# Three edits to the order of work in a hybrid mLSTM, retention and feed-forward block: gate tables stored head by head, one product's operands in step order, own buffers at its first gate

## The chip, the cores and the metric

The kernel runs on one core of one Trainium2 chip. The metric is the device time of one execution in microseconds (us); for several runs of one kernel the median is given. A profile is one execution taken by the hardware profiler. PE is TensorE's matmul part, PEld its weight load, DVE VectorE, ACT ScalarE, POOL GpSimd, SP SyncE, which issues most DMAs from one queue.

## The reference, cut to what matters

One block of a streaming encoder in float32: 16 meta tokens and 1024 positions of width 1024. A token mixer of four mLSTM heads and four retention heads (128 wide keys, 256 wide values, computed in chunks) is followed by an output product, and then by a gated feed-forward part with a causal convolution.

```
proj = up @ w_in                       # q, k, v, o, i, f and the retention's q, k, v, g
li = GATE_CAP * jnp.tanh(i_pre / GATE_CAP);  lf = jax.nn.log_sigmoid(ml_f + ml_b_f)
h_ml = mlstm_chunkwise(q, k, v, li, lf)      # stabilised by a running maximum of the gates
h_rt = retention_chunkwise(rq, rk, rv, log_gamma)
mixed = concat([sigmoid(ml_o) * head_norm(h_ml), silu(rt_g) * head_norm(h_rt)])
h = h + (mixed @ w_out)                      # the output product
...
a = causal_dwconv(u @ w_up, ffn_conv_w)      # u = rmsnorm(h)
h = h + (jax.nn.silu(a) * (u @ w_gate)) @ w_down
return rmsnorm(h, norm_final_g)[:, N_META:]
```

## The kernel before

Every product is kept exact to float32 by splitting each operand into a high part (a cast on ACT) and a low part (a subtraction on DVE), and by three matmuls for each pair of tiles: high by high, high by low, low by high. They are the lines 924 to 926 (`mm3s`), and every row `hi_x`, `lo_x`, `wr`, `rr`, `uh_g`, `ul_g` is such a half of a weight or an activation. Lines 783 and 784 (`wsplit`) split weights; line 1339 (`rsplit`) splits the output product's activations.

Large products use seven block products instead of eight, with sums and differences of blocks as operands. The output product (`mixw`, an instance of `Seven` with the name "w") goes through the stages "1", "65", "73", "4" and "2", each of eight steps k. A step of "65" or "73" has two products: 12 matmuls of 128x512 into four banks "y" and 12 into four banks "x". `prep` makes the operands of a step: in stage "65" it splits A1 (to `wr_01` at step 0), replaces A1 by -A1-B2 and splits that (`wr_00`), and then by -A1-A2 in place for a later stage. The second of two steps that share a ring has its activations in the tiles `rr`. The weight blocks' sums lie in DRAM (`wsw`) and come to `wdraw`'s tiles: two "raw" tiles, and two tiles `wd` with two places each. B1, A1 and so on are loaded from DRAM as well (`wa`).

The mLSTM heads need, for each head, two tables A1 and A2 that repeat a row of 1040 gate values on all 128 partitions. `gates` computes them for all heads and chunks as 36 rows (chunk times 4 plus head) of 128 and stores them in one DRAM tile `scr`; `tables_load` reads a head's rows back, broadcast to all partitions. The `raw_vp` loads bring weights of the value projection; their cast `hi_vp` stands on ACT (line 475). Line 1598 masks a chunk's scores (`pt`).

After the output product the rows are scaled by their root mean square, in three column ranges; `xcomb` then makes the combined operands for the feed-forward part's seven-product form (blocks `xh`, `uh_g`, `ul_g`). The first pair of the up and gate weights is done plainly in eight products, before all combinations exist: `first_up` and `first_gate`, with names such as `pup_000` (weight half m, column half, range) and `pga_11` (weight half m, column half). A gate's weight half is split into the hi/lo ring, which has three places.

The order of work is decided when the program is built: `watch` adds up estimated loads and end times of every instruction, the planner deals out tasks by them, and a scheduler orders each engine's instructions by simulated times, within the dependences. `after` adds an order without a semaphore between two instructions of one engine (a NoSync dependence). On each queue, SP's too, instructions go in the order in which they stand.

Of the kernel before, what the change touches and what calls it, by code (L numbers as in the profile page):

```python
# [17 lines left out]
P = 128  # L18
# [6 lines left out]
H = 4  # L25
# [64 lines left out]
def body(ctx, tc, h_in, vecs, cst, mask_in, rot, w_v0, w_vp, w_g, w_out, w_up, w_gate, w_down, out):  # L90
# [17 lines left out]
    last = {}  # L108
    G, PE, V, AC = nc.gpsimd, nc.tensor, nc.vector, nc.scalar
    pinned = [False]  # L110
    load = {"PE": 0.0, "DVE": 0.0, "Activation": 0.0, "Pool": 0.0, "SP": 0.0, "wire": 0.0}
    before = {}
    TABLES = ("Sqrt", "Sigmoid", "Silu", "Exp")
# [18 lines left out]
    def watch(ins):  # L132
        eng, kind = ins.engine.name, type(ins).__name__
        if "Tile" in kind or not ins.outs or eng not in load:
            return
        dma = "DMA" in kind
        seen[0] += 1
        if not dma and eng in ("PE", "DVE", "Activation"):
            if pinned[0] and eng in before:
                tc.add_manual_dep(ins, before[eng], mybir.DependencyInfo(mybir.DependencyClass.NoSync, mybir.DependencyReason.DATA), reason="order")  # L140
            before[eng] = ins.name
        o = ins.outs[0]
        n = math.prod(x[1] for x in o.ap[1:])
        rd = [e for e in map(extent, ins.ins) if e]
        wr = [e for e in map(extent, ins.outs) if e]
        t = load[eng]
        why = None
        for e, w in [(e, False) for e in rd] + [(e, True) for e in wr]:
            for lo, hi, wrote, at, by in uses.get(e[0], ()):
                if lo < e[2] and hi > e[1] and (w or wrote):  # L150
                    x = at if by == eng and not dma else at + 0.05
                    if by == eng and not dma:
                        continue
                    if x > t:
                        t, why = x, (by, e[0])
        if eng == "PE" and t - load["PE"] > 0.25:
            stalls.append((t, t - load["PE"], wr[0][0], why))
        if dma:
            load[eng] = t + (0.4 if eng == "SP" else 0.1)
            size = n * o.ap[0][1] * 4e-6  # L160
            if eng == "SP":
                load["wire"] = max(load["wire"], t + 1.8) + size / 0.3 * (2 if "scr" in str(rd) else 1)
                end = load["wire"]
            else:
                load["wire"] += size / 0.3
                end = t + 1.8 + size / 0.15
        else:
            if eng == "PE":
                if F32 not in [x.dtype for x in ins.ins]:
                    c = max(0.107, 0.004 + 0.000445 * n)  # L170
                elif o.ap[0][1] == 32:
                    c = 0.13
                elif getattr(ins, "is_transpose", False):
                    c = 0.109
                else:
                    c = 2 * max(0.11, 0.00084 * n)
                whole = F32 in [x.dtype for x in ins.ins]
                c += 0.1 * (whole != kindof[0])
                kindof[0] = whole
                end = t + c + 0.165  # L180
            elif eng == "DVE":
                c = 0.07 + 0.00105 * n + (0.06 if "ScalarPtr" in kind else 0.0)
                end = t + c + 0.085
            elif eng == "Activation":
                c = 0.045 + 0.00093 * n + 0.1 * (len(ins.ins) - 1)
                f = ins.func.name if hasattr(ins, "func") else "Copy"
                if f in TABLES and f != table[0]:
                    table[0] = f
                    c += 1.3
                end = t + c + 0.1  # L190
            else:
                c = 0.15 + 0.0017 * n
                end = t + c
            load[eng] = t + c
            fin[0] = max(fin[0], end)
        for e, w in [(e, False) for e in rd] + [(e, True) for e in wr]:
            u = uses.setdefault(e[0], [])
            if w:
                u[:] = [x for x in u if x[0] < e[1] or x[1] > e[2]]
            else:  # L200
                u[:] = [x for x in u if x[2] or x[4] != eng or x[0] < e[1] or x[1] > e[2]]
            u.append((e[1], e[2], w, end, eng if not dma else "q" + eng))
# [39 lines left out]
    gts = st.tile([P, 2, NCH, H], F32, name="gts")  # L242
    ug = st.tile([P, KB, 32], F32, name="ug")
    mask = st.tile([P, P], F32, name="mask")
    scr = dram.tile([2, R36, P], F32, name="scr")

    def sig(b, p):
        t0, t1, _ = PIECES[p]
# [530 lines left out]
    def wsplit(hi, lo, srcs):  # L779
# [5 lines left out]
            o += n  # L785
        return hi, lo

    def fstep(u, s):
        kind, i = fseq[u]
        nm = f"{kind}{i}_{s}"  # L790
        fetch(u)
        (w11, w12, r0), (w21, w22, r1) = fraws[u]
        if s:
            fetch(u + 1)
        if u < 2:
            return fsplit(nm, [(r0, r1)[s]])
        if s == 0:
            return fsplit(nm, [r0])
        if s == 1:
            s1 = fpool[0].tile([P, HB], F32, tag="s1", name=f"s1_{u}", bufs=1)  # L800
            V.tensor_tensor(s1, w21, w22, ALU.add)
            V.tensor_tensor(w21, w21, w11, ALU.subtract)
            V.tensor_tensor(w11, s1, w11, ALU.subtract)
            return fsplit(nm, [w11, s1])
        if s == 2:
            V.tensor_tensor(w12, w12, w11, ALU.subtract)
            return fsplit(nm, [w21, w12])
        return fsplit(nm, [w22])
# [338 lines left out]
    def tables_load(h):  # L1147
        if h <= H + 1:
            tabs[0], tabs[1] = (st.tile([P, 2 * SB], F32, tag=f"A{i + 1}", name=f"A{i + 1}_{h}") for i in range(2))
        A1, A2 = tabs[0][:, :T], tabs[1][:, :T]  # L1150
        if h > H + 1:
            return
        if h >= H:
            nc.sync.dma_start(A1, rot[:, 0])
            nc.sync.dma_start(A2, rot[:, 1])
            tabs["at"] = load["wire"]
            return
        src = scr.rearrange("x (c h) t -> x h c t", h=H)
        for x, a in ((0, A1), (1, A2)):
            if x == 0:  # L1160
                nc.sync.dma_start(a[:, :META], src[x, h, 0, :META].partition_broadcast(P))
            nc.sync.dma_start(a[:, META:].rearrange("p (c t) -> p c t", t=P), src[x, h, 1:].partition_broadcast(P))
        tabs["at"] = load["wire"]

    def tables_tasks(h):
# [76 lines left out]
    def gates():  # L1242
# [72 lines left out]
        V.tensor_scalar(mc[:, 1:2], mc[:, 1:2], math.log(KSCALE), None, ALU.add)  # L1315
        e, wi, ws = w, li, lf
        V.tensor_scalar(e, cm, mc[:, 0:1], -1.0, ALU.max, ALU.mult)
        nc.sync.dma_start(scr[0], e)
        AC.activation(wi, e, AF.Exp, bias=mc[:, 0:1])
        nc.sync.dma_start(scr[1], wi)  # L1320
        AC.activation(ws, t, AF.Exp, bias=mc[:, 1:2])
        V.tensor_tensor(b, e, b, ALU.subtract)
        AC.activation(b, b, AF.Exp, scale=2.0)
# [30 lines left out]
    class Seven:  # L1354
# [52 lines left out]
            return V.tensor_tensor(self.act[a, k], self.act[b, k], self.act[c, k], ALU.subtract)  # L1407

        def prep(self, t):

            if t >= len(self.steps) or t in self.ops:
                return
# [14 lines left out]
            elif st in self.QUARTER:  # L1427
                if k % 2 == 0:
                    self.w = fsplit(nm, [d["w"]])
                r = self.right.get((st, k)) or rsplit(act[{"1": "A1", "2": "A2", "4": "A1"}[st], k], self.rt(st, k, 0))  # L1430
                self.ops[t] = [(half_of(self.w, k % 2), r, "xy"[st == "2"])]
            elif st == "65":
                a1, a2, b2 = (act[q, k] for q in ("A1", "A2", "B2"))
                r5 = rsplit(a1, self.rt(st, k, 1))
                V.scalar_tensor_tensor(a1, a1, -1.0, b2, ALU.mult, ALU.subtract)
                w = fsplit(nm, [d["l"]])
                r6 = rsplit(a1, self.rt(st, k, 0))
                V.scalar_tensor_tensor(a1, a1, -1.0, a2, ALU.mult, ALU.subtract)
                self.ops[t] = [(half_of(w, 0), r6, "x"), (half_of(w, 1), r5, "y")]
            else:  # L1440
                w = fsplit(nm, [d["l"]])
                r7 = rsplit(act["B1", k], self.rt(st, k, 0))
                r3 = rsplit(act["B2", k], self.rt(st, k, 1))
                self.ops[t] = [(half_of(w, 1), r7, "x"), (half_of(w, 0), r3, "y")]
# [67 lines left out]
    wcount = {"draw": 0}  # L1512

    def wdraw(st, nm):
        if st == "1" or nm in ("w65_0", "w65_1", "w65_2", "w65_3"):
            left = next((q for q in jfreed if q), None)
            return raw_tile(nm, left.pop(0) if left and st == "1" else None)
        if not wdraws:
# [501 lines left out]
    def xcomb(k, j0, j1):  # L2020
# [3 lines left out]
        u4, t3, t2 = (xtile(f"x{x}{k}_{j0}", n) for x in "utv")  # L2024
        AC.activation(u4, B4, AF.Copy, scale=g4)
        x = V.scalar_tensor_tensor(t3, B1, g1, u4, ALU.mult, ALU.subtract)
        if k or j0:
            after(x, last["scaled"])
        V.scalar_tensor_tensor(t2, A1_, g1, t3, ALU.mult, ALU.subtract)
        xput(4, k, j0, j1, t2)  # L2030
# [219 lines left out]
    def eight(kind, half, j0, j1, bank, done):  # L2250
        for m in range(2):
            hi, lo = need((kind, 0, m), 2 - m)
            pt = bank(m)[:, :j1 - j0]
            xs = [xb(kb // 4 if half == 0 else (6, 2)[kb // 4]) for kb in range(KB)]
            mm3s(pt, [tuple(y[:, kb * P:(kb + 1) * P] for y in (hi, lo)) for kb in range(KB)],
                 [tuple(y[:, kb % 4, j0:j1] for y in xs[kb]) for kb in range(KB)], True, True)
            done(m, pt)

# [339 lines left out]
```

## Time and profile before

| | |
|---|---|
| median of 3 runs | 1526.14 us (1525.41 to 1527.58) |
| profiled execution, first to last instruction (span) | 1523.9 us |
| what the median has beyond that span | 2.2 us |
| mean granted TensorE clock | 0.995 |
| busy: PE, DVE, ACT, POOL | 98%, 72%, 50%, 5% |
| matmuls | 9929 |
| HBM read and written | 178.05 and 67.15 MB |

A row of the timeline reads: start in us, duration in us, engine, line of the kernel, operation, output<-inputs, shape, how many; in brackets the idle time of the engine just before, and what ended it. Matmuls overlap: the distance of two starts is what one costs, its duration is longer. In the view of stretches a row has the bounds, the length, busy time and count for PE, PEld, DVE, ACT and POOL, and at the end the granted clock, the share of the 16 DMA engines and GB/s. A row of the transfers gives size and median time from issue to landing.

### The profile page before, as it was taken

The page shows a single profiled execution, that of the slowest core. Times are in us where ns is not written, and L with a number is a line of the kernel's source. Part 1 is how long each engine was busy: PE and PEld are TensorE (multiplying, and loading weights), DVE is VectorE, ACT ScalarE, POOL GpSimd, SP SyncE. Part 2 cuts the span into 40 slices and gives each one's busy share as a digit, 9 for nine tenths or more (in the row PEclk, how much of TensorE's full clock was granted, in tenths as well). Part 3 has the DMA queues.
Part 4 walks back from the last instruction along what each step waited for, and adds up shares of the span by engine and source line. Part 5 has one row for each costly group of instructions (what it writes and reads, how often), then busy time and mean ns, then how long its engine had stood idle before and what let it go on. Part 6 is the DMA issues. An engine that isn't in the chain of part 4 may idle for free.

```text
span 1523.9 us, 25488 instructions
## 1 busy us (share of the span) xinstructions
PE 1487.8 (98%) x9929; PEld 1349.9 (89%) x9929; DVE 1090.4 (72%) x2087; ACT 756.4 (50%) x1455; POOL 72.1 (5%) x157
## 2 busy tenths in 40 slices
PE   7989999999999999999999999999999999999997
PEld 7988999998999999987888998999999999888887
DVE  6885868677777677756867787766666666778667
ACT  4465655554655455544454565444444444344443
POOL 1000000000000000000000001222220000000000
PEclk9999999999999999999999999999999999999999
DMA  6022245323632446697333247887772224933213
GB/s 232 2 93 56 90 155 192 111 84 111 200 106 98 131 161 199 194 401 258 108 115 125 77 136 222 209 211 201 177 186 77 83 82 157 369 106 108 97 42 111
DMA packets 104586, 223.81 MB, mean 147 GB/s; under 512 B 10520, under 2 KB 33760, under 8 KB 104288
## 3 DMA queue, kind: packets, MB, share of 16 engines
q1 hardware_dynamic: 89824, 191.68, 37.4%
q0 software_dynamic: 8448, 23.07, 7.6%
q10 hardware_dynamic: 6192, 7.41, 1.4%
q8 instruction: 78, 1.28, 0.3%
q14 instruction: 44, 0.36, 0.1%
HBM read 178.05 MB, written 67.15 MB: 161 GB/s over the span
## 4 chain that ended last, share of the span: by engine, by line
PE 89%; DVE 5%; ACT 2%; DMA 2%; issue 1%; SPq 0%; DVEq 0%; ACTq 0%
PE pdx L926 3%; PE pdx L925 3%; PE pdx L924 3%; PE pup_x L925 2%; PE pup_x L924 2%; PE pup_x L926 2%; PE pga_x L924 2%; PE pga_x L925 2%; PE pga_x L926 2%; PE pdy L926 2%; PE pdy L925 2%; PE pdy L924 2%; PE n L1621 2%; PE pwx L926 2%; PE u L1619 2%; PE pwx L924 2%
## 5 line engine op out<-in xcount | busy, mean ns | idle before, releaser
L783 ACT CAST hi_up<-raw_up 128x512 fp32r<-128x512 f32 (+1 forms) x52 | 36.4, 719 | 106.7 <-PE pga_z L925 60.2
L924 PE MATMUL pup_x<-uh_g,hi_up 128*128 128x256 f32 (+1 forms) x240 | 67.6, 284 | 1.2 <-ACT uh_g L1995 1.2
L784 DVE TENSOR_TENSOR lo_up<-raw_up,hi_up 128x512 fp32r<-128x512 f32 (+1 forms) x52 | 41.3, 809 | 38.3 <-ACT hi_up L783 37.5
L784 DVE TENSOR_TENSOR lo_ga<-fraw_ga,hi_ga 128x512 fp32r<-128x512 f32 (+1 forms) x52 | 41.9, 808 | 37.3 <-ACT hi_ga L783 37.1
L925 PE MATMUL pup_x<-ul_g,hi_up 128*128 128x256 f32 (+1 forms) x240 | 67.7, 284 | 0.1
L926 PE MATMUL pup_x<-uh_g,lo_up 128*128 128x256 f32 (+1 forms) x240 | 66.5, 283 | 0.0
L784 DVE TENSOR_TENSOR lo_d<-rd,hi_d 128x1024 fp32r<-128x1024 f32 (+1 forms) x34 | 37.7, 1113 | 32.8 <-ACT hi_d L783 32.7
L783 ACT CAST hi_ga<-fraw_ga 128x512 fp32r<-128x512 f32 (+1 forms) x52 | 36.4, 719 | 45.5 <-PE pup_z L925 24.1
L926 PE MATMUL pdx<-uh_d,lo_d 128*128 128x512 f32 (+1 forms) x156 | 57.9, 375 | 0.0
L925 PE MATMUL pdx<-ul_d,hi_d 128*128 128x512 f32 (+1 forms) x156 | 57.8, 374 | 0.0
L783 ACT CAST hi_d<-rd 128x1024 fp32r<-128x1024 f32 (+1 forms) x34 | 32.3, 959 | 49.3 <-PE pdy L925 32.5
L926 PE MATMUL pdy<-uh_d,lo_d 128*128 128x512 f32 x132 | 51.9, 393 | 0.0
L925 PE MATMUL pdy<-ul_d,hi_d 128*128 128x512 f32 x132 | 51.7, 392 | 0.0
L924 PE MATMUL pdx<-uh_d,hi_d 128*128 128x512 f32 (+1 forms) x156 | 48.5, 372 | 0.0
L924 PE MATMUL pdy<-uh_d,hi_d 128*128 128x512 f32 x132 | 47.9, 389 | 0.0
L924 PEld LDWEIGHTS pup_x<-uh_g,hi_up 128*128 128x128 f32 x240 | 45.7, 191 | 2.3 <-ACT uh_g L1995 1.4
L924 PE MATMUL pga_x<-uh_g,hi_ga 128*128 128x512 f32 x120 | 47.5, 396 | 0.0
L925 PE MATMUL pga_x<-ul_g,hi_ga 128*128 128x512 f32 x120 | 47.5, 396 | 0.0
L926 PE MATMUL pga_x<-uh_g,lo_ga 128*128 128x512 f32 x120 | 47.1, 393 | 0.0
L925 PEld LDWEIGHTS pup_x<-ul_g,hi_up 128*128 128x128 f32 x240 | 45.8, 191 | 1.0 <-DVE ul_g L1996 0.3
L926 PEld LDWEIGHTS pup_x<-uh_g,lo_up 128*128 128x128 f32 x240 | 45.0, 190 | 0.7
L1688 DVE SCALAR_TENSOR_TENSOR mx<-tr,vec,sig 128x386 f32<-128x386 f32 (+2 forms) x42 | 24.0, 571 | 21.1 <-PE tr L1680 16.0
(1687 smaller groups left out, 5732.4 us busy)
## 6 DMA issues: line engine op xcount, KB each, us to landing
raw_up<-w_up_d SPq DMA_DIRECT2D x22, 512.0 KB, 5.6
fraw_ga<-w_gate_d SPq DMA_DIRECT2D x22, 512.0 KB, 4.3
acts<-cv SPq DMA_DIRECT2D x44, 256.0 KB, 4.6
wsd<-w_down_d POOLq DMA_DIRECT2D x44, 256.0 KB, 6.7
rd<-wsd SPq DMA_DIRECT2D x22, 512.0 KB, 3.5
raw_w<-w_out_d SPq DMA_DIRECT2D x20, 512.0 KB, 7.3
wsw<-raw_w SPq DMA_DIRECT2D x32, 256.0 KB, 3.1
raw_m<-w_out_d SPq DMA_DIRECT2D x14, 512.0 KB, 4.0
```

The lines of the kernel that those rows point to most:

```text
L783: AC.copy(hi[:, o:o + n], x)
L784: V.tensor_tensor(lo[:, o:o + n], x, hi[:, o:o + n].bitcast(F32), ALU.subtract)
L924: m.append(PE.matmul(pt, ah, xh_, start=first and k == 0, stop=False, skip_group_check=True))
L925: PE.matmul(pt, ah, xl_, start=False, stop=False, skip_group_check=True)
L926: m.append(PE.matmul(pt, al, xh_, start=False, stop=last and k == n - 1, skip_group_check=True))
L1619: PE.matmul(up[:, :nv], kw[:L], v, start=True, stop=True)
L1621: PE.matmul(pn[:L, :nv], pt[:L, :L], v, start=True, stop=c == 0)
L1688: return V.scalar_tensor_tensor(dst, tr[:, x0 - t0:x1 - t0], vec[:, g:g + 1], sig(b, p)[:, x0 - a0:x1 - a0], ALU.mult, ALU.mult)
```

## The change

A. `scr` becomes eight DRAM tiles of 9 rows, one for each table and head. `gates` writes them with eight stores instead of two, after both row sets are there. A head's table is then one contiguous piece of 4 KB for each partition instead of eight pieces of 512 B.

B. `prep` of the stages "65" and "73" of the output product puts its PE, DVE and ACT instructions into a chain, one for each engine, in the order in which they are issued (`row`, `rows65`). In stage "65" the weight split stands ahead of the first activation split. `wdraw` gives the two raw tiles to the weights of the steps 4 to 7 of stage "65"; before, steps 0 to 3 had them.

C. At the first gate the second weight half is split into four tiles of the ring "cv" instead of the hi/lo ring (`wsplit2`); `eight` takes it as two pieces. In `xcomb` the order behind the last scaled row holds for the second column range alone, no longer for k > 0 of the first.

```diff
+            if row and eng in row[0]:
+                tc.add_manual_dep(ins, row[0][eng], mybir.DependencyInfo(mybir.DependencyClass.NoSync, mybir.DependencyReason.DATA), reason="order")
+            if row:
+                row[0][eng] = ins.name
...
-    scr = dram.tile([2, R36, P], F32, name="scr")
+    scr = [[dram.tile([NCH, P], F32, name=f"scr{x}{h}") for h in range(H)] for x in range(2)]
...
+    def wsplit2(nm, x):
+        r = [[ctile(f"{p}{nm}_{i}", F32R) for i in range(2)] for p in ("hi", "lo")]
+        for i in range(2):
+            wsplit(r[0][i], r[1][i], [x[:, i * HB:(i + 1) * HB]])
+        return r
...
+        if (u, s) == (1, 1):
+            return wsplit2(nm, r1)
...
-            nc.sync.dma_start(a[:, META:].rearrange("p (c t) -> p c t", t=P), src[x, h, 1:].partition_broadcast(P))
+            nc.sync.dma_start(a[:, META:], scr[x][h][1:].rearrange("c t -> (c t)").partition_broadcast(P))
...
-        nc.sync.dma_start(scr[0], e)
         AC.activation(wi, e, AF.Exp, bias=mc[:, 0:1])
-        nc.sync.dma_start(scr[1], wi)
+        for h in range(H):
+            for x, y in enumerate((e, wi)):
+                nc.sync.dma_start(scr[x][h], y[h:R36:H])
...
         def prep(self, t):
+            if self.nm == "w" and t < len(self.steps) and self.steps[t][0] in ("65", "73"):
+                row.append(rows65)
+                self.make(t)
+                row.clear()
+            else:
+                self.make(t)
...
                 a1, a2, b2 = (act[q, k] for q in ("A1", "A2", "B2"))
+                w = fsplit(nm, [d["l"]])
                 r5 = rsplit(a1, self.rt(st, k, 1))
                 V.scalar_tensor_tensor(a1, a1, -1.0, b2, ALU.mult, ALU.subtract)
-                w = fsplit(nm, [d["l"]])
                 r6 = rsplit(a1, self.rt(st, k, 0))
...
-        if st == "1" or nm in ("w65_0", "w65_1", "w65_2", "w65_3"):
+        if st == "1" or nm in ("w65_4", "w65_5", "w65_6", "w65_7"):
...
-        if k or j0:
+        if j0:
             after(x, last["scaled"])
```

PE's row order is the same as before up to stage "65". Three places show what moves. On SP's queue where the gate tables are stored (`scr`; in the new names scr_119 to scr_122 hold the first table of heads 0 to 3, scr_123 to scr_126 the second), before:

```order
L329 DMA raw_vp_22_1270<-w_vp_d 128x1024
L329 DMA raw_q0b<-w_g_d 128x512 x2
L1318 DMA scr<-gates 36x128
L1320 DMA scr<-gates 36x128
L1161 DMA A_0_1704<-scr 128x16
L1162 DMA A_0_1704<-scr 128x8x128
L1162 DMA A_0_1705<-scr 128x8x128
L329 DMA raw_vp_11_1266<-w_vp_d 128x1024
L329 DMA raw_vp_12_1304<-w_vp_d 128x1024
```

And on SP's queue at the same place now:

```order
L1333 DMA scr_125<-gates 9x128
L1333 DMA scr_122<-gates 9x128
L1333 DMA scr_126<-gates 9x128
L334 DMA raw_vp_11_1279<-w_vp_d 128x1024
L334 DMA raw_vp_12_1317<-w_vp_d 128x1024
L1173 DMA A_0_1717<-scr_119 128x16
L1174 DMA A_0_1717<-scr_119 128x1024
L1174 DMA A_0_1718<-scr_123 128x1024
L334 DMA raw_o0a<-w_g_d 128x1024
```

Head 0's two tables have moved behind the two raw_vp loads, which follow the eight stores directly.

On ACT at the start of stage "65" (hi_w_0 and so on are the weights of step 0 and on, wr_01 and wr_00 the activations of step 0, rr those of step 1, wr_21 those of step 2), before:

```order
L783 CAST hi_w_6_8323<-raw_w_6_8063 128x1024
L783 CAST hi_w_0_8418<-raw_w_0_8069 128x1024
L1339 CAST rr_8358<-wa_8375 128x512
L783 CAST hi_w_1_8448<-raw_w_1_8188 128x1024
L1339 CAST rr_8357<-wa_8375 128x512
L783 CAST hi_w_2_8488<-raw_w_2_8265 128x1024
L1339 CAST wr_01_8414<-wa_8375 128x512
L1339 CAST wr_00_8422<-wa_8375 128x512
```

And on ACT now:

```order
L788 CAST hi_w_6_8335<-raw_w_6_8076 128x1024
L788 CAST hi_w_0_8425<-wd_8082 128x1024
L1352 CAST wr_01_8429<-wa_8386 128x512
L1352 CAST wr_00_8433<-wa_8386 128x512
L788 CAST hi_w_1_8455<-wd_8082 128x1024
L1352 CAST rr_8369<-wa_8386 128x512
L1352 CAST rr_8368<-wa_8386 128x512
L788 CAST hi_w_2_8495<-wd_8083 128x1024
```

Step 0's activations have moved ahead of the weights of steps 1 and 2. On DVE, whose rows follow the same order, wr_01's low part now stands behind the last residual additions of stage "1" and the last mixing rows (`wa`, `mm`):

```order
L789 TENSOR_TENSOR lo_w_0_8426<-wd_8082,hi_w_0_8425 128x1024
L1709 SCALAR_TENSOR_TENSOR wa_8279<-tr_1_1_8331,vec,sig 128x126
L1709 SCALAR_TENSOR_TENSOR wa_8326<-tr_1_1_8331,vec,sig 128x258
L1496 TENSOR_TENSOR resid_8136<-resid_8136,pwx_8140 128x512
L1496 TENSOR_TENSOR resid_8136<-resid_8136,pwx_8144 128x512
L1496 TENSOR_TENSOR resid_8137<-resid_8137,pwx_8159 128x512
L1709 SCALAR_TENSOR_TENSOR wa_8326<-tr_2_0_8348,vec,sig 128x254
L1709 SCALAR_TENSOR_TENSOR mm<-tr_2_0_8348,vec,sig 128x2
L1496 TENSOR_TENSOR resid_8137<-resid_8137,pwx_8175 128x512
L1709 SCALAR_TENSOR_TENSOR wa_8326<-tr_2_1_8356,vec,sig 128x254
L1709 SCALAR_TENSOR_TENSOR mm<-tr_2_1_8356,vec,sig 128x2
L1352 TENSOR_TENSOR wr_01_8429<-wa_8386,wr_01_8429 128x512
```

Before, lo_w_1 and lo_w_2 and the first step-1 activation stood among these rows, ahead of wr_01's low part.

On PE at the first gate, before, the end of the gate's first product (pga_01) and what follows:

```order
L926 MATMUL pga_01_9855<-xh_9052,lo_ga_0_9732 128x512
L924 MATMUL pup_000_9911<-uh_g,hi_up_0_9418 128x256
L924 MATMUL pup_100_9938<-uh_g,hi_up_1_9426 128x256
L925 MATMUL pup_000_9911<-ul_g,hi_up_0_9418 128x256
L926 MATMUL pup_000_9911<-uh_g,lo_up_0_9419 128x256
```

And on PE now:

```order
L939 MATMUL pga_01_9872<-xh_9065,lo_ga_0_9745 128x512
L937 MATMUL pga_11_9900<-xh_9067,higa_1_0_9860 128x512
L938 MATMUL pga_11_9900<-xl_9068,higa_1_0_9860 128x512
L939 MATMUL pga_11_9900<-xh_9067,loga_1_0_9862 128x512
L840 MATMUL pcb_9646<-cs,Rb 128x1 x2
L937 MATMUL pga_11_9900<-xh_9067,higa_1_0_9860 128x512
```

The 24 matmuls of pga_11 have moved from behind the second column range of the up product to the front; pup_000, pup_100, pga_00 and pga_10 follow them, and the second range (pup_001 and on) comes after those.

More of the change, by code (lines that the diff above doesn't have):

```diff
@@ L110, in body @@
     pinned = [False]
+    row, rows65 = [], {}
     load = {"PE": 0.0, "DVE": 0.0, "Activation": 0.0, "Pool": 0.0, "SP": 0.0, "wire": 0.0}
@@ L1157, in tables_load @@
             return
-        src = scr.rearrange("x (c h) t -> x h c t", h=H)
         for x, a in ((0, A1), (1, A2)):
             if x == 0:
-                nc.sync.dma_start(a[:, :META], src[x, h, 0, :META].partition_broadcast(P))
-            nc.sync.dma_start(a[:, META:].rearrange("p (c t) -> p c t", t=P), src[x, h, 1:].partition_broadcast(P))
+                nc.sync.dma_start(a[:, :META], scr[x][h][0, :META].partition_broadcast(P))
+            nc.sync.dma_start(a[:, META:], scr[x][h][1:].rearrange("c t -> (c t)").partition_broadcast(P))
         tabs["at"] = load["wire"]
@@ L1409, in prep, with make @@
         def prep(self, t):
+            if self.nm == "w" and t < len(self.steps) and self.steps[t][0] in ("65", "73"):
[4 more added lines that the diff above has]
+                self.make(t)
+        def make(self, t):
             if t >= len(self.steps) or t in self.ops:
@@ L2254, in eight @@
             xs = [xb(kb // 4 if half == 0 else (6, 2)[kb // 4]) for kb in range(KB)]
-            mm3s(pt, [tuple(y[:, kb * P:(kb + 1) * P] for y in (hi, lo)) for kb in range(KB)],
+            mm3s(pt, [tuple(y[kb // 4][:, kb % 4 * P:(kb % 4 + 1) * P] if type(y) is list else y[:, kb * P:(kb + 1) * P] for y in (hi, lo)) for kb in range(KB)],
                  [tuple(y[:, kb % 4, j0:j1] for y in xs[kb]) for kb in range(KB)], True, True)
```

## The prediction

> **What bounds the kernel now.** I read the page first: busy shares, then the chain that ended last.
>
> ```profile
> span 1523.9 us, 25488 instructions
> ...
> PE 1487.8 (98%) x9929; PEld 1349.9 (89%) x9929; DVE 1090.4 (72%) x2087; ACT 756.4 (50%) x1455; POOL 72.1 (5%) x157
> ...
> PE 89%; DVE 5%; ACT 2%; DMA 2%; issue 1%; SPq 0%; DVEq 0%; ACTq 0%
> ```
>
> PE (TensorE) is busy for 1487.8 of 1523.9 us, so the change, which leaves the number of matmuls alone, can win at most the idle 36.1 us, and slow matmuls beside them. The view of PE's waits says which idle time lies where the change works (columns: microseconds in total, times, longest):
>
> ```profile
> PE s L1574 <- DVE pt L1598: 2.2, 1, 2.2
> PE pwy L925 <- DVE wr L1339: 1.8, 1, 1.8
> PE pup L925 <- DVE ul_g L1999: 1.7, 1, 1.7
> ...
> PE pwy L924 <- ACT wr L1339: 1.3, 1, 1.3
> ...
> PE pup_x L924 <- ACT uh_g L1995: 1.2, 1, 1.2
> ...
> PE pga L924 <- ACT hi_ga L783: 0.8, 1, 0.8
> ```
>
> These six are one wait near the tables, two (1.8 and 1.3) at the start of stage "65" of the output product, three (1.7, 0.8, 1.2) around the first gate: 9.0 us. Then the granted clock, by stretches (the column before the last two):
>
> ```profile
> 120.00:130.00 10.00, 7.77 (x54) 7.19 (x53) 5.23 (x15) 3.56 (x9) 0.00 (x0) 1.00 0.25 98
> 710.00:720.00 10.00, 10.00 (x38) 8.00 (x37) 4.66 (x8) 3.17 (x5) 0.00 (x0) 0.83 0.70 263
> 720.00:730.00 10.00, 10.00 (x45) 8.11 (x44) 7.99 (x11) 4.01 (x6) 0.00 (x0) 1.00 0.35 107
> 870.00:880.00 10.00, 8.31 (x68) 7.97 (x67) 8.17 (x23) 4.95 (x12) 0.00 (x0) 1.00 0.00 0
> 920.00:930.00 10.00, 10.00 (x71) 9.66 (x70) 8.08 (x14) 6.12 (x13) 1.76 (x3) 0.92 0.46 158
> ```
>
> From 710 to 720 PE is "busy" throughout, but issues 38 matmuls where the next stretch issues 45, at a clock of 0.83; 920 to 930 shows 0.92. A wait there costs more than its idle time.
>
> **Part A, tables stored head by head.** It turns 2 stores into 8 and two loads of 8 pieces a partition into loads of one; what counts is that on SP's queue the two raw_vp loads now stand ahead of head 0's tables. Today they stand behind them:
>
> ```profile
> 108.54 0.55 SPq L1320 DMA_DIRECT2D scr<-gates  x1
> 112.55 9.76 DMA raw_vp<-w_vp_d
> 122.34 1.14 ACT L475 CAST hi_vp<-raw_vp 128x512 fp32r<-128x512 f32 x2 [4.74 <-DMA raw_vp<-w_vp_d]
> 123.77 0.35 DVE L1598 SCALAR_TENSOR_TENSOR pt<-s,cs 128x128 f32<-128x128 f32 x1 [4.43 <-ACT kw L1590]
> 160.94 0.17 DVE L1174 TENSOR_TENSOR A<-A,mask 128x16 f32<-128x16 f32 x1
> A<-scr SPq DMA_DIRECT2D x2, 512.0 KB, 8.1
> raw_o0a<-w_g_d SPq DMA_DIRECT2D x1, 512.0 KB, 4.3
> ```
>
> The raw_vp transfer takes 9.76 us behind 1 MB of tables (8.1 us each); ACT stands 4.74 us in front of its cast, with kw behind it, then pt on DVE, and PE waits 2.23 us. Without the tables ahead I take the 4.3 us of raw_o0a, the next load of that size: landing at 116.9, 5.4 us earlier, and the 2.23 us go as long as it lands within 7.5 us. The stores: eight issues from 108.54 on at 0.55 us end at 112.9 at the worst, and with the first of them sent earlier at 112.4; the raw_vp loads went out at 112.55 for their buffer's sake, so the stores cost nothing, at worst 0.4 us. Head 0's tables now go out at some 114.6 and are first read at 160.94; even at 9.76 us they are hidden. So the layout itself, one piece of 4 KB instead of eight of 512 B, buys no time that I can see; later heads' tables have even more room. Between -0.4 and 2.2 us I take **2.0**, near the upper end, since that is a load of the same size from the same queue.
>
> **Part B, stage "65" in step order.** Rows of PE, DVE and ACT at the start of the stage, and two of the transfers from 686 to 780:
>
> ```profile
> 706.27 1.56 PE L924 MATMUL pwy<-wr,hi_w 128*128 128x512 f32 x4 [1.34 <-ACT wr L1339]
> 709.60 0.50 PE L925 MATMUL pwy<-wr,hi_w 128*128 128x512 f32 x1 [1.78 <-DVE wr L1339]
> ...
> 713.82 0.40 PE L924 MATMUL pwy<-rr,hi_w 128*128 128x512 f32 x1
> ...
> 715.69 0.40 PE L926 MATMUL pwy<-rr,lo_w 128*128 128x512 f32 x1
> 705.41 0.68 DVE L1475 TENSOR_TENSOR resid<-resid,pwx 128x512 f32<-128x512 f32 x1
> 706.61 0.48 DVE L1688 SCALAR_TENSOR_TENSOR wa<-tr,vec,sig 128x254 f32<-128x254 f32 x1
> ...
> 707.73 1.22 DVE L784 TENSOR_TENSOR lo_w<-raw_w,hi_w 128x1024 fp32r<-128x1024 f32 x1
> 708.86 0.69 DVE L1339 TENSOR_TENSOR wr<-wa,wr 128x512 fp32r<-128x512 f32 x1
> 703.18 1.06 ACT L783 CAST hi_w<-raw_w 128x1024 fp32r<-128x1024 f32 x1 [6.50 <-issue]
> raw_w<-wsw SPq DMA_DIRECT2D x2, 512.0 KB, 4.8
> wm<-w_out_d SPq DMA_DIRECT2D x1, 1024.0 KB, 9.5
> ```
>
> PE is free at 704.93 (706.27 less 1.34). ACT has cast wr_01 only by then, behind the weights of steps 1 and 2, the first of which it starts at 703.18; DVE makes its low part only at 708.86, behind lo_w of steps 1 and 2 (1.22 each). Now wr_01 stands on ACT behind hi_w of step 0 alone, so it falls into the 6.50 us that ACT idles ahead of 703.18, and the 1.34 us go. On DVE the row order is lo_w of step 0, four residual adds, the two mixes, then wr_01: the last residual add can't start before PE's last matmul of stage "1", about 704.75; 0.60 for it and 0.52 for the mix and mm (0.68 and 0.48 in the rows, which overlap a little) put wr_01's low part at 705.87 to 706.56. PE's first four matmuls (no low part needed) run from 704.92 to 705.85: a wait of 0.7 is left. So 1.34 + 1.78 - 0.7 = 2.4 us. Then the clock: 11 matmuls from 709.60 to 713.82 took 4.22 us, while 8 from 713.82 to 715.69 took 0.234 each, so 11 should take 2.57: 1.65 us lost, which I count as won, since only 0.7 us of idle time is left there.
>
> Does the strict order starve a later step? A step has 24 matmuls, 24 x 0.234 = 5.6 us of PE. DVE owes it lo_w 1.13 (by the spacing 707.73 to 708.86), and four or five 512-wide operations at 0.6 to 0.69: 3.5 to 4.6 us; ACT has 4.01 of 10 us to do in 720:730. So PE outruns neither; by the rows in order, operands are ready 1.5 to 2 us before their matmuls at steps 1 and 2. The weights of steps 4 to 7 now take the two raw tiles, so those of 6 and 7 load when the low parts of 4 and 5 are done, about 726 and 731.5; at 4.8 us for such a load (9.5 for the slowest of this stretch, of twice the size) step 6's is there at 731 to 735.5, and PE comes at 704.9 + 6 x 5.6 = 738.5. Part B: bounds 0 (other waits take over) and 4.8 (no wait left); I take **4.0**.
>
> **Part C, the first gate.** Its second weight half has tiles of its own, so its cast needn't wait for a ring slot; 24 matmuls of the early half (pga_11) move in front of the up product.
>
> ```profile
> 866.58 0.40 PE L924 MATMUL pup<-uh_g,hi_up 128*128 128x256 f32 x2
> 871.80 2.77 DVE L2070 TENSOR_TENSOR resid<-resid,Rb 128x256 f32<-128x256 f32 x8 [3.59 <-ACT Rb L843]
> 880.48 1.04 ACT L783 CAST hi_ga<-fraw_ga 128x1024 fp32r<-128x1024 f32 x1 [0.92 <-PE pup L925]
> 913.99 0.69 DVE L2283 TENSOR_TENSOR cv<-s0ga,cv 128x512 f32<-128x512 f32 x1 [0.97 <-ACT cv L2241]
> 916.37 0.39 PE L924 MATMUL pup_x<-uh_g,hi_up 128*128 128x258 f32 x1 [1.19 <-ACT uh_g L1995]
> ...
> 917.51 0.28 PE L926 MATMUL pup_x<-uh_g,lo_up 128*128 128x258 f32 x1
> ...
> 918.21 0.36 PE L926 MATMUL pup_z<-uh_g,lo_up 128*128 128x256 f32 x1
> ...
> 921.59 0.34 PE L925 MATMUL pup_x<-ul_g,hi_up 128*128 128x258 f32 x1
> ```
>
> Today PE does pup of the first quarter from 866.58 and runs into the second quarter's operands, which the scaling chain (871.80, then ul_g) has not made: 1.69 us. With 5.6 us of pga_11 first, and the first quarter's up and gate (96 matmuls at 0.117, as between 917.51 and 918.21, 11.2 us) behind it, the second quarter comes due at 883.4. Its chain: PE's row broadcast stands 12 matmuls into the up product, at 873.6; a microsecond for ACT's copy, the eight scalings (2.77) and ul_g behind them end at 879. The 1.69 go; so do the 0.78, since the cast at 880.48 no longer waits for PE. The first scaling chain gets two low parts (2 x 0.6) ahead of it on DVE; it is due 5.6 us later, so that is free. At 916.37 PE waits for the last combined operands. DVE's 3.59 us of idle time ahead of 871.80 now hold the first half of the combinations, so that queue is shorter by about 5 us behind a chain that starts 2.7 later, while PE comes 2.5 us sooner. The multiply at 913.99 still waits for ACT ahead of the last combination; I leave 0.3 of the 1.19. Behind it, three matmuls from 916.37 to 917.51 took 1.14 instead of 0.35; 0.5 of these 0.79 go. The half clock: 16 matmuls from 918.21 to 921.59 took 3.38; at the 0.117 of the six from 917.51 to 918.21 it is 1.87: 1.5 us, won. Sum 2.47 + 0.9 + 0.5 + 1.5 = 5.4; with 0.2 for operands that now come late, **5.2**. Bounds 0 and 5.9.
>
> **Sum.** 2.0 + 4.0 + 5.2 = 11.2: the profiled span goes from 1523.9 to 1512.7. The median of the runs, 1526.14, stands 2.2 above the span, so 1514.9, say **1515 us**. All three upper ends give 12.9, or 1513.2. No wait of the list above lies behind 917, so what is won stays won.
>
> The Trainium skill weighs against the clock term: "TensorE: Matmul & The Clock Gate", Part 1, says that the clock falls to half only after at least one idle window of about 3.4 us, so gaps of 1.2 to 1.8 us would cost their idle time alone. The trace has 0.83 directly behind gaps of 1.34 and 1.78 us, hence I follow the row.
>
> **The rivals.**
> - The clock term is not tied to these waits. The lone gap of 1.69 us left 1.00 in 870:880, and the one of 2.23 left 1.00 in 120:130, so a gap does not always halve the clock; the half stretches could come from elsewhere and stay. Then 11.2 - 1.65 - 1.5 = 8.0: 1518.1. By the page's rule above, this would be the case. Against it: both stretches begin at a wait.
> - DVE stays late at the last combinations (its share is 8.08 of 10 us in 920:930). The wait before the first combined product stays at 1.2 or more, with its half clock: 11.2 - 0.9 - 0.5 - 1.5 = 8.3, 1517.8.
> - No gain: PE arrives sooner, and the transfers it then needs are paced by others (0.70 DMA share in 710:720), so that the waits reappear; 1525 to 1526. Part A alone could do nothing if the raw_vp loads were slow by themselves.
> - Slower: the strict order in stages "65" and "73" makes DVE wait in line. 16 steps; a step has 5.6 us of PE and up to 4.6 of DVE, so each microsecond over 1.0 that DVE stands still per step is PE time. Two stages at 2.0 us of waiting cost 16 x 1.0 = 16 us, against 11.2 won: 1531. It decides from 1.7 us a step. DVE's 7.99 of 10 us in 720:730 says there is room for it, but nothing in the rows in order asks for such a wait.
>
> **How the numbers follow.** Forecast 0.65 (its own range 1513 to 1517), clock term elsewhere 0.10, late combinations 0.12, no gain 0.07, slower 0.06. Differences under 0.2%, 3 us, can't be told from none. Faster: 0.65 + 0.10 + 0.12 = 0.87; within 0.2%: 0.07; slower: 0.06. The range runs from 1512, a little under all upper ends, to 1521, which takes in both rivals near 1518 and one part failing beside them.
>
> **What would show it.** A: no PE wait near 124, raw_vp landing in 4 to 5 us. B: one wait under 1 us at about 705, and a clock of 1.00 in the 10 us behind it. C: no waits of PE on ul_g and hi_ga, a wait under 0.5 us on the combined operands, clock 1.00 behind it. The prediction is wrong if a wait over 1 us stands inside stages "65" or "73", if the half-clock stretches come without waits before them, or if raw_vp still takes over 7.5 us.

## The result, and the profile after

The changed kernel takes 1514.6 us (median of 4 runs, 1513.15 to 1515.7) against 1526.18 us before; the ratio is 0.9922, 95% interval 0.991 to 0.9934. That is 11.6 us faster, with 11.2 forecast. Most single terms of the sum came out otherwise than forecast, though, and their errors cancelled, so that the closeness of the total is partly luck. One execution of B alone (2595.75 us) and one of C alone (8304.02) were in a far slower state; the ratios and intervals below leave them out.

The page of the profiled execution after, then PE's waits:

```profile
span 1513.8 us, 25492 instructions
...
PE 1484.5 (98%) x9929; PEld 1347.9 (89%) x9929; DVE 1090.2 (72%) x2088; ACT 755.1 (50%) x1456; POOL 72.2 (5%) x157
...
PE 92%; DVE 4%; ACT 2%; DMA 1%; issue 1%; SPq 0%; DVEq 0%; ACTq 0%
```

```profile
PE pwy L938 <- DVE wr L1352: 1.6, 1, 1.6
...
PE tr L1701 <- DVE mx L1709: 1.5, 1, 1.5
...
PE pwy L937 <- DVE mm L1709: 0.5, 1, 0.5
```

Of the six waits of before (9.0 us), those on pt, ul_g, hi_ga and uh_g are gone. The two at the start of stage "65" have become the 0.5 us. The 1.6 us are new. The wait of `tr` on `mx` was there before with 1.2 us and varies from execution to execution. Stretches after, with the same columns as before:

```profile
100.00:110.00 10.00, 10.00 (x64) 9.80 (x64) 6.93 (x25) 6.35 (x13) 0.19 (x1) 0.73 0.01 3
120.00:130.00 10.00, 10.00 (x70) 9.50 (x69) 6.15 (x17) 3.88 (x10) 0.00 (x0) 1.00 0.23 91
710.00:720.00 10.00, 10.00 (x45) 8.14 (x44) 8.39 (x13) 5.33 (x8) 0.00 (x0) 1.00 0.67 251
870.00:880.00 10.00, 10.00 (x87) 10.00 (x86) 9.59 (x26) 6.55 (x18) 0.00 (x0) 1.00 0.08 28
920.00:930.00 10.00, 10.00 (x49) 8.25 (x48) 7.82 (x12) 4.62 (x9) 2.36 (x3) 1.00 0.99 282
```

The clock is 1.00 at 710 and at 920. But 100 to 110 has 0.73 in this execution, where it had 0.88 before. PE's order is the same there, and the slow matmuls end at 105.3, ahead of the first of the eight stores (108.41):

```profile
100.00:110.00 10.00, 10.00 (x74) 9.80 (x74) 7.26 (x26) 6.54 (x14) 0.19 (x1) 0.88 0.03 6
```

To say where time went, I compare the starts of the same matmuls. Before, then after:

```profile
98.27 0.19 PE L1290 MATMUL pe<-cs,gates 36*1 36x36 f32 x1 [1.55 <-DVE gates L1283]
...
113.81 0.29 PE L1574 MATMUL s<-qT,kT 128*128 128x16 f32 x2
...
127.39 0.38 PE L1574 MATMUL s<-qT,kT 128*128 128x128 f32 x2
...
704.54 0.38 PE L1680 MATMUL tr<-cs,n 128*128 128x128 f32 x2
...
831.55 1.17 PE L827 MATMUL pcb<-cs,Rb 128*128 128x1 f32 x10
...
950.54 0.28 PE L924 MATMUL pup_z<-uh_g,hi_up 128*128 128x256 f32 x1
```

```profile
98.23 0.19 PE L1302 MATMUL pe<-cs,gates 36*1 36x36 f32 x1 [1.56 <-DVE gates L1295]
...
115.11 0.29 PE L1595 MATMUL s<-qT,kT 128*128 128x16 f32 x2
...
126.18 0.38 PE L1595 MATMUL s<-qT,kT 128*128 128x128 f32 x2
...
703.65 0.38 PE L1701 MATMUL tr<-cs,n 128*128 128x128 f32 x2
...
827.88 1.17 PE L840 MATMUL pcb<-cs,Rb 128*128 128x1 f32 x10
...
940.42 0.28 PE L937 MATMUL pup_z<-uh_g,hi_up 128*128 128x256 f32 x1
```

Subtracting neighbours: the gates' stretch (pe to the first s) takes 15.54 and then 16.88 us, the next (to the fifth chunk's s, part A) 13.58 and 11.07, the heads 577.15 and 577.47, stages "65" to "2" (tr to pcb, part B) 127.01 and 124.23, the rest up to pup_z (part C) 118.99 and 112.54. In these two executions A gave 2.5 us, B 2.8, C 6.4; the clock near 100 took 1.3 back and the heads 0.3: 10.1, the difference of the spans. The medians differ by 1.5 us more.

### The profile page after: what moved, and what is told of

The parts are those of the page before. It is cut to its first block, busy times and chain, and to the rows that moved or that the text cites. A ratio compares the mean times of both kernels' runs of the same rounds, so it can differ in the third digit from the quotient of the medians.

```text
span 1513.8 us, 25492 instructions
## 1 busy us (share of the span) xinstructions
PE 1484.5 (98%) x9929; PEld 1347.9 (89%) x9929; DVE 1090.2 (72%) x2088; ACT 755.1 (50%) x1456; POOL 72.2 (5%) x157
## 4 chain that ended last, share of the span: by engine, by line
PE 92%; DVE 4%; ACT 2%; DMA 1%; issue 1%; SPq 0%; DVEq 0%; ACTq 0%
PE pdx L939 3%; PE pdx L938 3%; PE pdx L937 3%; PE pup_x L938 3%; PE pup_x L937 3%; PE pup_x L939 3%; PE pga_x L937 2%; PE pga_x L938 2%; PE pga_x L939 2%; PE pdy L939 2%; PE pdy L938 2%; PE pdy L937 2%; PE n L1642 2%; PE pwx L939 2%; PE pwx L938 2%; PE pwx L937 2%
```

## The experiments

Each kernel is compared with the kernel before on the same chip. Four stretches of each profile are given by the starts of the matmuls above (us):

| kernel | median, before beside it | ratio, 95% interval | pe to first s | pe to fifth s (A) | tr to pcb (B) | pcb to pup_z (C) |
|---|---|---|---|---|---|---|
| before | | | 15.54 | 29.12 | 127.01 | 118.99 |
| changed | 1514.6, 1526.18 | 0.991 to 0.9934 | 16.88 | 27.95 | 124.23 | 112.54 |
| A alone | 1522.88, 1526.64 | 0.9969 to 0.9986 | 15.62 | 26.69 | 128.26 | 117.68 |
| A's order, old layout | 1522.93, 1526.64 | 0.9969 to 0.9986 | 16.93 | 28.00 | 126.96 | 117.61 |
| B alone | 1524.82, 1526.64 | 0.9976 to 0.9993 | 15.64 | 30.57 | 124.19 | 119.05 |
| C alone | 1518.75, 1526.64 | 0.9935 to 0.996 | 14.99 | 29.18 | 127.00 | 112.57 |
| changed again | 1514.08, 1526.37 | 0.9904 to 0.9931 | 15.65 | 26.73 | 124.19 | 112.53 |
| chain in "65" only | 1515.09, 1526.37 | 0.991 to 0.9935 | 14.98 | 26.06 | 124.97 | 112.55 |
| additions later | 1513.29, 1526.37 | 0.9898 to 0.9925 | 15.51 | 26.58 | 123.16 | 112.58 |
| C, own buffers only | 1525.54, 1526.37 | 0.9985 to 1.0003 | 14.99 | 30.70 | 127.01 | 117.34 |
| B, chain only | 1524.37, 1525.8 | 0.9983 to 1.0001 | 15.00 | 30.87 | 124.23 | 119.13 |
| C, freed order only | 1526.26, 1525.8 | 0.9996 to 1.0013 | 14.99 | 30.78 | 127.00 | 117.53 |

**A alone.** The diff's part A on the kernel before.

```diff
-    scr = dram.tile([2, R36, P], F32, name="scr")
+    scr = [[dram.tile([NCH, P], F32, name=f"scr{x}{h}") for h in range(H)] for x in range(2)]
```

> Part A alone on the kernel before. If the gain of A is the wait of PE on pt near 124 us, that wait goes and the time falls by 2.2 to 2.5 us (-0.15%), all other waits as before. Rival: the eight stores and the later tables cost something elsewhere (head 0's tables late at 161 us, other heads' loads), then PE shows a new wait between 124 and 400 us and the time falls by less than 1.5 us.

The time fell by 3.8 us, more than I expected (the interval, 2.1 to 4.7, takes in the 2.2 to 2.5), and the wait of 2.2 us on pt is gone. No wait of PE that wasn't there before stands between 124 and 400 us.

**A's order with the old layout.** One table tile with the rows and the loads of before, but eight stores:

```diff
-        nc.sync.dma_start(scr[0], e)
-        nc.sync.dma_start(scr[1], wi)
+        for h in range(H):
+            for x, y in enumerate((e, wi)):
+                nc.sync.dma_start(scr[x].rearrange("(c h) t -> h c t", h=H)[h], y[h:R36:H])
```

> The old DRAM table with its rows in the old order and the old loads of eight 512 B pieces a partition, but written by eight stores, so that on SP's queue the raw_vp loads stand ahead of head 0's tables as in the changed kernel. If the order on the queue makes the gain of A: -2.2 to -2.5 us, as for A alone, and the tables of heads 0 to 3 still land in about 8 us. Rival: the contiguous layout makes it, then the wait near 124 us stays in part and the time is within 1 us of the kernel before.

It fell by 3.7 us, like A alone, and from the first to the fifth chunk's s both take 11.07 us. The queue's order makes the gain; the contiguous layout adds nothing that shows. How long the tables take to land, which I had also forecast, isn't in this trace. The eight stores aren't free, though. SP's queue in the changed kernel, and the cast behind it:

```profile
108.41 6.01 SPq L1333 DMA_DIRECT2D scr<-gates  x8
114.52 0.89 SPq L334 DMA_DIRECT2D raw_vp<-w_vp_d  x2
118.91 1.14 ACT L480 CAST hi_vp<-raw_vp 128x512 fp32r<-128x512 f32 x2
L1333 SPq DMA_DIRECT2D scr<-gates x8: 675/684/852, 108.4 to 113.7; - x8
```

A store of 9 rows holds SP for 0.68 us (the last row has least, median and most in ns), where the ones of 36 rows took 0.38 and 0.55. The raw_vp loads go out at 114.52, and not when DVE is done with their buffer at 112.84. They land before ACT comes to them at 118.91 (no wait in that row). In four of the six profiles with A, where ACT comes sooner, it does stand 0.5 to 1.0 us in front of that cast; the longest is with the chain in "65" only, a version described below:

```profile
113.47 0.88 SPq L334 DMA_DIRECT2D raw_vp<-w_vp_d  x2
...
117.83 1.14 ACT L480 CAST hi_vp<-raw_vp 128x512 fp32r<-128x512 f32 x2 [1.03 <-DMA raw_vp<-w_vp_d]
```

There the loads are in 4.4 us after the first of them was issued. PE waits for it in none of the six: all take 11.07 or 11.08 us from the first to the fifth chunk's s. So the 1.7 us are hidden from PE.

**B alone.** The diff's part B on the kernel before.

```diff
+            if self.nm == "w" and t < len(self.steps) and self.steps[t][0] in ("65", "73"):
+                row.append(rows65)
...
-        if st == "1" or nm in ("w65_0", "w65_1", "w65_2", "w65_3"):
+        if st == "1" or nm in ("w65_4", "w65_5", "w65_6", "w65_7"):
```

> Part B alone on the kernel before. By the trace of the changed kernel: the start of stage 65 wins 4.3 us (3.1 of waits down to 0.5, and the half clock of 1.65), and a new wait of 1.6 us stands at the change from stage 65 to 73, so -2.8 us. If the half clock does not hang on the two waits, 710 to 720 us still shows about 0.83 and the gain is 1.1 us. If the new wait comes from the other parts, it is missing here and the gain is 4.3 us.

The stretch of B is 2.8 us shorter, the median 1.8 (interval 1.1 to 3.7). 710 to 720 us has a clock of 1.00, and the new wait of 1.6 us is there, so it belongs to B:

```profile
PE s L1587 <- DVE pt L1611: 2.0, 1, 2.0
...
PE pwy L930 <- DVE wr L1344: 1.6, 1, 1.6
...
710.00:720.00 10.00, 10.00 (x45) 8.12 (x44) 8.36 (x12) 4.91 (x8) 0.00 (x0) 1.00 0.91 324
```

**C alone.** The diff's part C on the kernel before.

```diff
+        if (u, s) == (1, 1):
+            return wsplit2(nm, r1)
...
-        if k or j0:
+        if j0:
```

> Part C alone on the kernel before. By the trace of the changed kernel: the three waits around the first gate go (1.7, 0.8, 1.2 us) with the half clock behind 918 us: -6.4 us. If the half clock behind 918 is a matter of phase and not of the wait, it stays and the gain is 4.9 us or less. If the last combined operands depend on what A and B do earlier, a wait of about 1 us stays there.

The three waits are gone, the clock is 1.00 at 910 to 930, and the stretch takes 112.57 us, as in the changed kernel. The median fell by 7.9 us (interval 6.1 to 9.9); the stretch accounts for 6.4 of it.

**The changed kernel again, and two versions of its chain.** The first has no edit.

> The changed kernel once more, beside the two below. The parts alone sum to 3.5 + 2.3 + 7.9 = 13.7 us less; if they are independent, this one is 11.5 to 13.7 us faster than the kernel before. Its profile again has the new wait of 1.6 us at the change from stage 65 to 73; the stretch behind 99 us may have none, one or two half-clock windows of 3.4 us, if these are a matter of phase.

12.3 us faster than the kernel before; the parts alone sum to 3.8 + 1.8 + 7.9 = 13.5. The wait of 1.6 us is there again, and behind 99 us there is one stretch of half clock this time. What stands on DVE in front of that wait (the changed kernel's profile):

```profile
745.29 1.29 DVE L1496 TENSOR_TENSOR resid<-resid,pwy 128x512 f32<-128x512 f32 x2 [3.02 <-PE pwy L939]
746.50 0.69 DVE L1352 TENSOR_TENSOR rr<-wa,rr 128x512 fp32r<-128x512 f32 x1
747.10 0.69 DVE L1420 TENSOR_TENSOR wa<-wa,wa 128x512 f32<-128x512 f32 x1
747.70 1.28 DVE L1496 TENSOR_TENSOR resid<-resid,pwy 128x512 f32<-128x512 f32 x2
748.90 0.69 DVE L1459 SCALAR_TENSOR_TENSOR wa<-wa,wa 128x512 f32<-128x512 f32 x1
749.50 1.22 DVE L789 TENSOR_TENSOR lo_w<-wd,hi_w 128x1024 fp32r<-128x1024 f32 x1
750.63 1.28 DVE L1352 TENSOR_TENSOR wr<-wa,wr 128x512 fp32r<-128x512 f32 x2
...
751.98 0.50 PE L938 MATMUL pwy<-wr,hi_w 128*128 128x512 f32 x1 [1.59 <-DVE wr L1352]
```

DVE idles 3.02 us in front of a residual addition that needs PE's last matmul into its bank, and the low parts of stage "73"'s step 0 stand behind it. The second version chains stage "65" alone:

```diff
-            if self.nm == "w" and t < len(self.steps) and self.steps[t][0] in ("65", "73"):
+            if self.nm == "w" and t < len(self.steps) and self.steps[t][0] in ("65",):
```

> The changed kernel, but only stage 65's operands are chained, not those of stage 73. If the new wait at the change of stage comes from the chain (stage 73's first low parts stand behind residual additions that wait for PE), it is gone or under 0.5 us, and the time is 1 to 1.6 us below the changed kernel's. Rival: DVE simply has too much to do there, with eight residual additions of 0.6 us; then a wait of 1 us or more stays in any order.

The wait on wr is gone, but two others on ACT have come, and the stretch takes 124.97 us, 0.8 more than the changed kernel's:

```profile
PE pwx L937 <- ACT rr L1352: 2.0, 2, 1.2
```

So neither expectation held as it was meant. A wait of over 1 us stays (1.2), which was the rival's sign, but it is on ACT's casts to `rr` and not on DVE's additions. The third version puts the additions behind those low parts, bank y's first:

```diff
+            ordered = self.nm == "w" and st == "65"
-            for b, j0, half in self.GIVE[st]:
+            for b, j0, half in self.GIVE[st][::-1 if ordered else 1]:
...
-                    V.tensor_tensor(x, x, self.banks[b, j], ALU.subtract if j0 else ALU.add)
+                    m = V.tensor_tensor(x, x, self.banks[b, j], ALU.subtract if j0 else ALU.add)
+                    if ordered:
+                        tc.add_manual_dep(m.ins, rows65["DVE"], mybir.DependencyInfo(mybir.DependencyClass.NoSync, mybir.DependencyReason.DATA), reason="order")
+                        rows65["DVE"] = m.ins.name
```

> The changed kernel with one more piece in the chain: the eight residual additions at the end of stage 65 come behind the low parts of stage 73's step 0, and those of bank y before those of bank x. DVE's idle time of 3.0 us in front of the first addition should then hold these low parts, and the wait of 1.6 us falls to 0.3 or less: 1.3 to 1.6 us below the changed kernel. Rival: the additions now come late, and PE waits for bank y instead, about 1 us; then no gain.

The wait falls from 1.6 to 0.5 us, now on a cast to `rr`, and the stretch from 124.19 to 123.16, somewhat less than the 1.3 to 1.6 expected:

```profile
PE pwy L937 <- ACT rr L1352: 0.5, 1, 0.5
```

Its median, 1513.29, is the lowest of all, but stands only 0.8 below the changed kernel's on the same chip, inside the spread of the runs (1512.67 to 1514.69 and 1513.6 to 1515.04).

**Halves of B and C.** B's chain without the exchange of tiles; against B alone:

```diff
-        if st == "1" or nm in ("w65_4", "w65_5", "w65_6", "w65_7"):
+        if st == "1" or nm in ("w65_0", "w65_1", "w65_2", "w65_3"):
```

> Part B without the exchange of the weights' tiles: steps 0 to 3 of stage 65 keep the two raw tiles, which for steps 2 and 3 load only when the low parts of steps 0 and 1 are done. If the chain makes the gain: as B alone, -2 to -2.8 us. If the exchange is needed: in step order the low part of step 1 comes at about 710 us, so step 3's weights load from then on, land by 715 to 720, and are due at 721; a wait of PE there would show it, at most 2 us, and the gain would be under 1 us.

Its stretch of B, 124.23 us, is that of B alone. The chain, together with the weight split ahead of the first activation split, which this version keeps, makes the gain; the exchange adds nothing here, and none of the waits on weights that I had thought possible appears. Which of the two orders counts for how much, no run separates. C's own buffers without the freed order; against C alone:

```diff
-        if j0:
+        if k or j0:
             after(x, last["scaled"])
```

> Of part C only the own buffers for the second weight half; the combinations stay behind the last scaled row. If the order of the gate product in front of up makes the gain: the waits of 1.7 and 0.8 us go, the one on the last combined operands stays at 1 us or more: -3 us. If freeing the combinations is what matters, less than -1.5 us. If both are needed only for the last wait: that wait grows, since DVE now starts its combinations after a later scaling.

And the freed order without the buffers; against C alone:

```diff
-        if (u, s) == (1, 1):
-            return wsplit2(nm, r1)
```

> Of part C only the freed combinations: the first quarter's combinations may stand ahead of the second scaling, the gate keeps its ring slot and its place. PE's order is that of the kernel before. If the early gate product is what covers the second scaling: the wait of 1.7 us grows, since six more operations (0.4 to 0.5 us each) stand on DVE ahead of that scaling, of which 3.6 us of idle time covers most; 1.5 to 2.5 us for this wait, the one on the last combined operands shrinks from 1.2 to below 0.5, so between -1.5 and +0.5 us in all.

Alone, each is within the noise: -0.8 and +0.5 us (the interval of the first still allows a gain of 2.3). With the buffers only, the waits of 1.7 and 0.8 us are gone, but the last one splits in two, with a stretch of half clock behind them in this execution (0.85 in 910 to 920):

```profile
PE pup_x L932 <- ACT uh_g L2003: 1.1, 1, 1.1
...
PE pup_z L932 <- ACT uh_g L2006: 0.7, 1, 0.7
```

With the freed order only, all three waits stay as they were. DVE does seven more operations ahead of the second scaling (I had counted six), but in time in which it was idle:

```profile
873.13 2.77 DVE L2070 TENSOR_TENSOR resid<-resid,Rb 128x256 f32<-128x256 f32 x8 [0.89 <-ACT Rb L843]
```

The idle time in front of this row falls from 3.59 to 0.89, and the row still waits for ACT's copy: so the wait on ul_g neither grew, as I had expected, nor shrank. And the last column range's `xt`, which the last combined operands need, still stands behind the multiply that waits 0.97 us for ACT, so the last wait didn't shrink below 0.5 us as expected. With the buffers only it stands there too. With both halves, in the changed kernel, it is ahead of that multiply:

```profile
904.65 0.48 DVE L2047 SCALAR_TENSOR_TENSOR xt<-resid,vec,xv 128x258 f32<-128x258 f32 x1
...
906.12 0.69 DVE L2304 TENSOR_TENSOR cv<-s0ga,cv 128x512 f32<-128x512 f32 x1 [0.66 <-ACT cv L2262]
```

Only both halves together get the last combination through in time.

## Why the prediction was right, point by point

**A, 2.0 forecast.** The mechanism held, the size didn't. The mean of "pe to fifth s" is 30.2 us over the six profiles without A and 27.0 over the six with it: 3.2 us. That is rather too little, since the profiles with A happen to have more half clock ahead of the first s (15.9 us from pe to first s on average, against 15.2): among profiles with one stretch of half clock there the difference is 3.2, among those with none 4.3 (a single profile with A), and the medians gave 3.8 and 3.7. Whether A has a part in that half clock, twelve profiles can't tell; nothing of A stands ahead of it on PE. The step that failed is the one that took PE's wait of 2.23 us from one execution. In that one, half-clock matmuls near 100 us had held PE back, and the wait hid it: raw_vp lands when its own chain allows. Where PE came early it waited longer, and the clock could drop behind the wait, as it did in four of the six profiles without A. With C's freed order alone (PE's wait, then two stretches):

```profile
PE s L1574 <- DVE pt L1598: 2.9, 1, 2.9
...
100.00:110.00 10.00, 9.21 (x77) 8.76 (x75) 7.26 (x25) 6.78 (x15) 0.19 (x1) 1.00 0.03 6
120.00:130.00 10.00, 7.13 (x39) 6.43 (x38) 4.58 (x13) 2.78 (x7) 0.00 (x0) 0.83 0.23 91
```

Wrong too was the step on the stores: it let them end by 112.9, at 0.55 us each, but they held SP until 114.4. It cost ACT up to 1.0 us and PE nothing. That raw_vp lands in 4 to 5 us without the tables ahead (4.4 measured), and that the layout buys nothing, was right.

**B, 4.0 forecast, 2.8 measured** (3.0 by the means: 127.2 over the six profiles without the chain, among them one of 128.3 with a longer half clock, and 124.2 over the four with all of it). The start of the stage came as forecast: 0.5 of wait left (0.7 forecast), the half clock gone. The step that failed is "PE outruns neither": DVE's work was counted for a step inside the stage, 3.5 to 4.6 us, and the eight residual additions at its end (0.6 us each, 4.8 us) were left out, as was the order among them and stage "73"'s first low parts. That is the 1.6 us wait, at step 0 of stage "73", and by the forecast's own list of signs (no wait over 1 us inside "65" or "73") this part was wrong. That it comes from that order, and not from the amount of work, is shown by the version with the additions later. The rival in which DVE makes PE wait in line came true at one of sixteen steps.

**C, 5.2 forecast, 5.9 measured** (118.5 us over the five profiles with none of C, 112.6 over the five with all of it). The residue of 0.3 us that I left at the last combination did not come. The half clock behind it was counted as 1.5; it is there in only three of the six profiles that have the wait of 1.2 us (before, B alone, B's chain; not with A alone, A's order or C's freed order), so on average it is worth half that. Without it the stretch is 5.1 us shorter with C (117.68 with A alone, 112.57 with C alone). PE's idle time there goes from 3.82 to 0.04 us, which is the three waits; the other 1.3 is busy time. Of that, 0.5 lies in the first matmuls behind the last wait, as forecast (three matmuls that took 1.14 us take 0.66); the rest I put down to slow first matmuls behind the other two waits, which no run isolates.

**The rival on the clock** (its term not tied to these waits) came half true. At stage "65" it is tied: all six profiles without the chain have half-speed matmuls behind the two waits, and none of the six with it. At the gate it came in three of six profiles with the same wait; what decides it, the runs don't show.

The Trainium skill's rule, "TensorE: Matmul & The Clock Gate", Part 1, that the clock drops only after at least one idle window of about 3.4 us, does not hold here: waits of 1.3 and 1.8 us, with four matmuls between, did it in all six profiles. That section's window length and its remark that the window runs freely do agree with these runs: the half clock at the gate before lasts from 918.21 to 921.59, 3.38 us, and the same waits near 98 us gave no, one or two windows of half speed, by 14.98 to 15.00, 15.51 to 15.65 and 16.88 to 16.93 us for the same matmuls.

The rival with late combinations and the one with no gain did not come true. In sum, by the means, 3.2 + 3.0 + 5.9 = 12.1 us was there to be had, against 11.2 forecast: A and C were taken too small, B too large. That these errors nearly cancel is luck.

## What to carry to other kernels

When instructions are put into a strict order, cost the seams between stages as well as a step inside one: what a stage gives away at its end (here eight additions) shares the queue with the first operands of the next. A wait read from one execution is only as long as the engine in front of it was early; look how early that was before counting the wait as the gain. Two halves of an edit can each stay within the noise and together win 6 us, if they take away waits that follow each other on one chain.

## What the runs showed of the hardware

One piece of code with the same waits (1.66 us at 91, 1.55 and 0.77 at 98 to 99) ran at full clock, or with one or two stretches of half clock behind it, in different executions: 14.98, 15.5 or 16.9 us. That alone can make 1.9 us between two executions; 29 runs of the kernel before on one chip went from 1523.35 to 1528.24 us. A store of 9 rows of 512 B held SP's queue for 0.68 us, one of 36 rows for 0.38 to 0.55.
